# A hybrid decoder layer on one core: every fourth feed-forward weight tile gets its low part from an adding transfer

## The chip, the core and the metric

The kernel runs on one core of a Trainium2 chip. The metric is the device time of one execution in microseconds (us), lower being better. The engines are TensorE (PE; its weight loads are listed as PEld), VectorE (DVE), ScalarE (ACT), GpSimd (POOL) and SyncE (SP), which issues nearly all of the transfers. A transfer is carried out by 16 DMA engines that all queues share.

## The reference

One decoder layer over 256 tokens of width 2048, all in float32.

```
h = RMSNorm(x);  P = h @ W_in                  # pool channels (1024) | q | k | v (8 heads of 128 each)
A = pool_mixer(P_pool);  B = dilated_attention(q, k, v)
x = x + concat(RMSNorm(A), RMSNorm(B)) @ W_out
x = x + relu(RMSNorm(x) @ W_up)^2 @ W_down     # 8192 feed-forward columns
out = RMSNorm(x)
```

The feed-forward weights W_up and W_down are 64 MiB each, two thirds of what is read.

## The kernel before

**Products in three parts.** A float32 product a @ w runs as a_hi @ w_hi + a_lo @ w_hi + a_hi @ w_lo, where hi is the operand rounded to float32r and lo the exact rest. The activations' parts are made where the activations arise. The weights' parts are made tile by tile while the kernel runs.

**The weights' pipeline.** All weights are one list `order` of 176 tiles of 1 MiB (128 partitions x 2048 float32), in the order in which they are used: 32 for the input projection, 16 for the output projection, then four times 16 of W_up and 16 of W_down. A tile's index is t. Half a tile (128x1024) is one step s, with t = s // 2. In form B (used for W_up) a tile holds 8 row blocks of 256 columns and the weights are stationary; in form A (W_down) it holds 4 row blocks of 512 columns and the activations are stationary. Either way a step is 24 blocks of 512 columns' worth of products, or 8 pairs of a 512- and a 256-column product.

**The loop.** One Python loop goes over all the steps and writes the program of every engine. In iteration s it writes:

- `split(s + AHEAD)`, with `AHEAD` = 4: ScalarE rounds the half tile into `w_hi` (line 124), VectorE subtracts that from the raw half into `w_lo` (line 125). Both come from a pool with AHEAD + 1 = 5 buffers, so the high part of step s + 4 takes the buffer that the products of step s - 1 have just left.
- on even s, `load(s // 2 + RAW_AHEAD + 1)`, with `RAW_AHEAD` = 3: SyncE issues the transfer of a whole raw tile (line 108) into one of four buffers, once the tile that was in it has been split.
- `products(s)`: TensorE's products (lines 163 to 165 in form A, 169 and 171 in form B). In both forms the first product of a step reads `w_hi` and the second `w_lo`.
- the evacuation of an accumulator that is complete: for W_up `evac_up` by way of `joined` (lines 190, 192, 433, 435, 436, on ScalarE and VectorE in turn, every fourth step), for W_down `evac_down` (line 444, on VectorE, every eighth).

Each engine works through its program in the order written, and engines wait for each other by semaphores. Nothing is reordered.

**Buffers named `v0` and `v1`.** `v_parts`, the values of the attention, lie in the two buffers `v0` and `v1`. After the attention `v0` is used again for the gain of the last norm, `gfin` (lines 530 and 533), and `v1` for nothing more. GpSimd issues five small loads at the start (lines 68 to 500) and adds squares; it has nothing to do in the feed-forward part.

Of the kernel before, what the change touches and what calls it, by code (L numbers as in the profile page):

```python
# [8 lines left out]
F32R = mybir.dt.float32r  # L9
AF = mybir.ActivationFunctionType  # L10
OP = mybir.AluOpType
AX = mybir.AxisListType

P = 128
S = 256
# [17 lines left out]
@with_exitstack  # L33
def hybrid_block(ctx: ExitStack, tc: tile.TileContext, xT, x, w_v, w_qkp, w_out, w_up, w_down,
                 pool_w, pool_scale, g_mix, g_cat, g_mlp, g_final, ident_in, negdist_in, lncount_in, out):
    """Products of float32 operands a @ w run as a_hi @ w_hi + a_lo @ w_hi + a_hi @ w_lo, where hi is the
    operand rounded to float32r and lo the exact rest.  Form A keeps activations stationary and streams
    512 columns of weights (tokens on the output's partitions); form B keeps weights stationary and
    streams [a_hi | a_lo] (columns on the output's partitions)."""
    nc = tc.nc  # L40
    ctx.enter_context(tc.manual_schedule())

# [1 line left out]
    big = ctx.enter_context(tc.tile_pool(name="big", bufs=1))  # L44
    wraw = ctx.enter_context(tc.tile_pool(name="wraw", bufs=RAW_AHEAD + 1))
    wsplit = ctx.enter_context(tc.tile_pool(name="wsplit", bufs=AHEAD + 1))
    work = ctx.enter_context(tc.tile_pool(name="work", bufs=2))
# [4 lines left out]

    st = {}

    # ---- the scalar engine's square-root table, ahead of its first use
    warm = const.tile([P, 1], F32, name="warm")
    nc.vector.memset(warm, 1.0)
    nc.scalar.activation(warm, warm, AF.Sqrt)

    # ---- the tensor engine's clock comes up with work: products of zeros while the first loads are on their way  # L60
    zeros = const.tile([P, 256], mybir.dt.bfloat16, name="zeros")
    nc.vector.memset(zeros, 0.0)
    idle = ps_tp.tile([P, 256], F32, name="tp")
# [3 lines left out]
    gmix = const.tile([P, KT], F32, name="gmix")  # L67
    nc.gpsimd.dma_start(gmix, g_mix)

    # ---- operands in two parts: [row block, part, token]  # L70
    h_op = big.tile([P, KT, 2, S], F32R, name="h_op", tag="setA")
    xt = big.tile([P, KT, S], F32, name="xt", tag="setB")

# [3 lines left out]
                                       op0=OP.mult, op1=OP.subtract)  # L77

    def rsqrt_mean(ssq, n, name):
        """1 / sqrt(ssq / n + eps), with one Newton step behind the table's square root."""  # L80
        width = ssq.shape[-1]
        m = small.tile([P, width], F32, name=name + "_m", tag="rs_m%d" % width)
        nc.vector.tensor_scalar(m, ssq, 1.0 / n, EPS, op0=OP.mult, op1=OP.add)
        s = small.tile([P, width], F32, name=name + "_s", tag="rs_s%d" % width)
        nc.scalar.activation(s, m, AF.Sqrt)
        r0 = small.tile([P, width], F32, name=name + "_r0", tag="rs_r0%d" % width)
        nc.vector.reciprocal(r0, s)
        t = small.tile([P, width], F32, name=name + "_t", tag="rs_t%d" % width)
        nc.vector.tensor_tensor(t, r0, r0, op=OP.mult)
        nc.vector.tensor_tensor(t, t, m, op=OP.mult)  # L90
        nc.vector.tensor_scalar(t, t, -0.5, 1.5, op0=OP.mult, op1=OP.add)
        r = const.tile([P, width], F32, name=name)
        nc.vector.tensor_tensor(r, r0, t, op=OP.mult)
        return r

    # ---- the weights' pipeline: tiles of 1 MiB, split in halves
    order = []
    raws, splits, accs, tasks = {}, {}, {}, {}

    def load(t, pieces=1, of=None):  # L100
        if t >= len(order):
# [8 lines left out]
    def split(s, pieces=1, of=None, by_vector=False):  # L110
        t, half = divmod(s, 2)
        if t >= len(order):
            return
        src = raws[t][:, half * 1024:(half + 1) * 1024]
        if s not in splits:
            splits[s] = (wsplit.tile([P, 1024], F32R, name="w_hi"), wsplit.tile([P, 1024], F32R, name="w_lo"))
        hi, lo = splits[s]
        n = 1024 // pieces
        for i in of or range(pieces):
            c = slice(i * n, (i + 1) * n)  # L120
            if by_vector:
                nc.vector.tensor_copy(hi[:, c], src[:, c])
            else:
                nc.scalar.activation(hi[:, c], src[:, c], AF.Copy)  # L124
            nc.vector.tensor_tensor(lo[:, c], src[:, c], hi[:, c].bitcast(F32), op=OP.subtract)  # L125

    whole, halves = (slice(0, CA),), (slice(0, CA // 2), slice(CA // 2, CA))

    def cuts_of(key, tt):
        """The very last accumulator, of the second tile of tokens, comes in halves, each a tile by itself."""  # L130
        return halves if tt == 1 and key == order[-1]["key"] else whole

    def sums(key, tt, cut):
# [50 lines left out]
        tasks.setdefault(step, []).append((f, a))  # L184

    def joined(key):
        """Form B's sums: both halves of the accumulator together, [P, 2, S]."""
        acc = accs.pop(key)
        cross = work.tile([P, 2, S], F32, name="cross", tag="cross")
        nc.scalar.activation(cross, acc[:, :, S:], AF.Copy)  # L190
        z = work.tile([P, 2, S], F32, name="z", tag="z")
        nc.vector.tensor_tensor(z, acc[:, :, :S], cross, op=OP.add)  # L192
        return z

    # ---- input projection
    def square_x(n):
        """Squares of four row blocks, in the place of x, folded into one block and added to the others'."""
        t = xt[:, n * 4:n * 4 + 4]
        nc.scalar.activation(t, t, AF.Square)
        nc.gpsimd.tensor_tensor(t[:, :2], t[:, :2], t[:, 2:], op=OP.add)  # L200
        if n == 0:
            st["sq", "x"] = const.tile([P, S], F32, name="sq_x")
            nc.gpsimd.tensor_tensor(st["sq", "x"], t[:, 0], t[:, 1], op=OP.add)
        else:
            for i in range(2):
                nc.gpsimd.tensor_tensor(st["sq", "x"], st["sq", "x"], t[:, i], op=OP.add)  # L206
# [4 lines left out]
        nc.vector.tensor_scalar(st["rq"], st["r", "x"], SCALE, None, op0=OP.mult)  # L211

    def spread_rx():
        """The tokens' factors along the free dimension, on all partitions."""
        p = ps_tp.tile([P, S], F32, name="tp")
        for tt in range(TT):
            nc.tensor.transpose(p[:, tt * P:(tt + 1) * P], st["r", "x"][:, tt:tt + 1].to_broadcast([P, P]), ident)
        st["rrow"] = const.tile([P, S], F32, name="rrow")
        nc.vector.tensor_copy(st["rrow"], p)
# [83 lines left out]
        return st["y"]  # L303

    def squares(name, src, scale, first):
        """Sums of squares over row blocks, token by token, one sum to a partition."""
        if first:
            st["sq", name] = const.tile([P, S], F32, name="sq_" + name)
            nc.scalar.activation(st["sq", name], src, AF.Square, scale=scale)
        else:  # L310
            t = work.tile([P, S], F32, name="sqt", tag="sqt", bufs=1)
            nc.scalar.activation(t, src, AF.Square, scale=scale)
            nc.gpsimd.tensor_tensor(st["sq", name], st["sq", name], t, op=OP.add)
# [51 lines left out]
            base, f = {"p": (0, evac_pool), "q": (4, evac_qk), "k": (8, evac_qk)}[kind]  # L365
            add_b(lambda i, n=base + n: w_qkp[n, i], (kind, n), h_operand, f)

    # ---- output projection, of the two mixers by themselves, and the second norm's operand
    def load_rows():
        st["xr"] = [big.tile([P, D], F32, name="xr", tag="late%d" % tt) for tt in range(TT)]  # L370
        for tt in range(TT):
            nc.sync.dma_start(st["xr"][tt], x[tt * P:(tt + 1) * P, :])
# [50 lines left out]
        for c in range(4):  # L423
            add_a(lambda kq, c=c: w_out[c, kq], (name, c), kqs, y_op, evac_out)

    # ---- the feed-forward layer, 2048 of its columns at a time; the norm's factor, squared, comes last
    def evac_up(step, key):
        b, c = key[1:]
        if c == 0:
# [24 lines left out]
        for c in range(4):  # L454
            add_a(lambda kq, b=b, c=c: w_down[b, c, kq], ("d", b, c), range(4), lambda b=b: st["act", b], evac_down)

    # ---- start
    def load_xT(k0, n):
        nc.sync.dma_start(xt[:, k0:k0 + n], xT[:, k0:k0 + n, :])

# [15 lines left out]
    put_xT(0, 1)  # L476
    put_xT(1, 1)
    split(0, pieces=2, of=(1,))
    put_xT(2, 2)
    split(1, pieces=2)  # L480
# [60 lines left out]
    at(n_in + 68, halve_final)  # L541

    def finish(tt, cuts):
        """The last columns of a tile of tokens, and its final norm."""
        xr = st["xr"][tt]
        ss = st["ss2"][:, tt]
        base = D - CA
# [7 lines left out]
        last = ss[:, 2 + len(cuts):3 + len(cuts)]  # L555
        m = small.tile([P, 1], F32, name="m_end", tag="m_end")
        nc.vector.tensor_scalar(m, last, ss[:, 2:3], 1.0 / D, op0=OP.add, op1=OP.mult)
        s = small.tile([P, 1], F32, name="s_end", tag="s_end")
# [2 lines left out]
        nc.vector.reciprocal(r0, s)  # L561
        t = small.tile([P, 1], F32, name="t_end", tag="t_end")
        nc.vector.scalar_tensor_tensor(t, r0, r0, m, op0=OP.mult, op1=OP.mult)
        # -2 / sqrt(m): the gain carries -1/2
        r = small.tile([P, 1], F32, name="r_end", tag="r_end")
        nc.vector.scalar_tensor_tensor(r, t, -3.0, r0, op0=OP.add, op1=OP.mult)
        for n, (c0, c1) in enumerate(((0, 256), (256, 768), (768, 1280), (1280, 1536), (1536, 2048))):
# [8 lines left out]
            nc.sync.dma_start(out[tt * P:(tt + 1) * P, cols], xr[:, cols])  # L576

    def sum_early():
        """All of the final norm's sums but the last chunk's, with the epsilon."""
        ss = st["ss2"]  # L580
        nc.vector.tensor_tensor(ss[:, :, 2:3], ss[:, :, 2:3], ss[:, :, 1:2], op=OP.add)
        nc.vector.scalar_tensor_tensor(ss[:, :, 2:3], ss[:, :, 0:1], D * EPS, ss[:, :, 2:3], op0=OP.add, op1=OP.add)
# [4 lines left out]
    for s in range(n_steps - tail):  # L587
# [4 lines left out]
        t, half = divmod(s, 2)  # L592
# [6 lines left out]
            f(*a)  # L599
    assert not tasks  # L600

    # ---- the last products go by tiles of tokens, so that the first tile's norm and store run under the second's
    for s in range(n_steps - tail, n_steps):
        products(s, tts=(0,), drop=False)
    finish(0, whole)
# [57 lines left out]
```

## Time and profile before

| | |
|---|---|
| median of 2 runs | 1024.0 us (1022.86 and 1025.13) |
| span of the profiled execution | 1022.8 us; the page gives no other time of it |
| TensorE busy | 1007.7 us, 99% |
| VectorE busy | 626.1 us, 61% |
| ScalarE busy | 481.5 us, 47% |
| GpSimd busy | 30.9 us, 3% |
| moved by DMA | 194.26 MB, mean 190 GB/s |

The busy time of an engine says how much of the span it worked, with TensorE's ends modelled. Which engine sets the time is read from the chain that ended last and from the waits: the first follows the last instruction back through whatever released each step, the second adds up for each pair of instructions how long the one waited for the other.

### The profile page before, as it was taken

How to read it: one execution, taken by the hardware profiler on the slowest of the kernel's cores; microseconds unless marked ns; L12 is line 12 of the kernel's file. 1: busy time of each engine (PE TensorE's matmuls, PEld its weight loads, DVE VectorE, ACT ScalarE, POOL GpSimd, SP SyncE). 2: the span in 40 equal slices, each digit the busy share in tenths (PEclk: the TensorE clock that was granted, in tenths of full speed). 3: DMA queues.
4: the chain of work that ended last, by engine and by line, in shares of the span. 5: the costliest groups of instructions: out<-in, count | busy, mean ns of one | idle time of the engine just before them, and what ended most of it. 6: DMA issues, size and time to landing. Idle time of an engine off the chain costs nothing.

```text
span 1022.8 us, 12969 instructions
## 1 busy us (share of the span) xinstructions
PE 1007.7 (99%) x5208; PEld 858.8 (84%) x5208; DVE 626.1 (61%) x749; ACT 481.5 (47%) x612; POOL 30.9 (3%) x52
## 2 busy tenths in 40 slices
PE   9899999999999999999999999999999999999996
PEld 6788888888888888888888888888888888888886
DVE  7677866867676655555555545455655555565563
ACT  7456445464555445343444443444443434454442
POOL 2500010010000000000000000000000000000000
PEclk9899999999999999999999999999999999999999
DMA  9654454466455566555455555555555555555532
GB/s 333 243 207 174 138 201 170 160 234 219 165 183 188 177 221 220 189 186 202 170 201 186 186 206 186 187 188 184 202 173 197 206 185 186 186 186 198 178 118 83
DMA packets 30891, 194.26 MB, mean 190 GB/s; under 512 B 3504, under 2 KB 4576, under 8 KB 8304
## 3 DMA queue, kind: packets, MB, share of 16 engines
q1 hardware_dynamic: 30672, 193.34, 53.5%
q8 instruction: 41, 0.67, 0.3%
q0 software_dynamic: 160, 0.09, 0.1%
q14 instruction: 18, 0.15, 0.0%
HBM read 191.33 MB, written 2.10 MB: 189 GB/s over the span
## 4 chain that ended last, share of the span: by engine, by line
PE 95%; DMA 2%; POOL 2%; SPq 0%; ACT 0%; DVE 0%; issue 0%; DVEq 0%; POOLq 0%; ACTq 0%
PE acc L169 32%; PE acc L171 16%; PE acc L163 15%; PE acc L164 15%; PE acc L165 15%; DMA raw<-w_v_dram 1%; POOL sq_x L206 1%; POOL xt L200 1%; DMA xt<-xT_dram 1%; PE end L164 0%; PE end L165 0%; PE end L163 0%; PE tp L393 0%; PE tp L282 0%; PE sc L346 0%; PE sc L348 0%
## 5 line engine op out<-in xcount | busy, mean ns | idle before, releaser
L125 DVE TENSOR_TENSOR w_lo<-raw,w_hi 128x1024 fp32r<-128x1024 f32 (+1 forms) x360 | 431.6, 1215 | 258.6 <-ACT w_hi L124 258.6
L124 ACT ACTIVATE w_hi<-raw 128x1024 fp32r<-128x1024 f32 (+1 forms) x359 | 366.5, 1038 | 293.8 <-PE acc L165 184.1
L169 PE MATMUL acc<-x_op,w_hi 128*128 128x512 f32 x1024 | 360.4, 397 | 0.0
L171 PE MATMUL acc<-x_op,w_lo 128*128 128x256 f32 x1024 | 287.4, 281 | 0.0
L169 PEld LDWEIGHTS acc<-x_op,w_hi 128*128 128x128 f32 x1024 | 192.2, 188 | 46.5
L171 PEld LDWEIGHTS acc<-x_op,w_lo 128*128 128x128 f32 x1024 | 193.5, 189 | 0.2
L164 PE MATMUL acc<-w_lo,act 128*128 128x512 f32 x496 | 193.1, 389 | 0.0
L163 PE MATMUL acc<-w_hi,act 128*128 128x512 f32 x496 | 193.0, 389 | 0.0
L165 PE MATMUL acc<-w_hi,act 128*128 128x512 f32 x496 | 193.0, 389 | 0.0
L169 PE MATMUL acc<-h_op,w_hi 128*128 128x512 f32 x384 | 138.0, 402 | 0.0
L165 PEld LDWEIGHTS acc<-w_hi,act 128*128 128x128 f32 x496 | 93.1, 188 | 19.5
L163 PEld LDWEIGHTS acc<-w_hi,act 128*128 128x128 f32 x496 | 93.1, 188 | 19.1
L164 PEld LDWEIGHTS acc<-w_lo,act 128*128 128x128 f32 x496 | 93.1, 188 | 18.9
L171 PE MATMUL acc<-h_op,w_lo 128*128 128x256 f32 x384 | 108.3, 282 | 0.0
L169 PEld LDWEIGHTS acc<-h_op,w_hi 128*128 128x128 f32 x384 | 73.4, 191 | 16.7
L171 PEld LDWEIGHTS acc<-h_op,w_lo 128*128 128x128 f32 x384 | 73.7, 192 | 0.1
L190 ACT ACTIVATE cross<-acc 128x512 f32<-128x512 f32 x44 | 26.2, 596 | 67.0 <-PE acc L171 67.0
L192 DVE TENSOR_TENSOR z<-acc,cross 128x512 f32<-128x512 f32 x44 | 30.4, 691 | 42.6 <-ACT cross L190 42.6
L163 PE MATMUL acc<-w_hi,y_op 128*128 128x512 f32 x128 | 50.6, 396 | 0.0
L165 PE MATMUL acc<-w_hi,y_op 128*128 128x512 f32 x128 | 50.0, 390 | 0.0
L164 PE MATMUL acc<-w_lo,y_op 128*128 128x512 f32 x128 | 49.9, 390 | 0.0
L435 ACT ACTIVATE act<-z 128x512 fp32r<-128x512 f32 x32 | 20.3, 633 | 47.5 <-DVE z L433 47.5
(169 smaller groups left out, 613.6 us busy)
## 6 DMA issues: line engine op xcount, KB each, us to landing
raw<-w_up_dram SPq DMA_DIRECT2D x64, 1024.0 KB, 4.7
raw<-w_down_dram SPq DMA_DIRECT2D x64, 1024.0 KB, 4.8
raw<-w_qkp_dram SPq DMA_DIRECT2D x24, 1024.0 KB, 4.8
raw<-w_out_dram SPq DMA_DIRECT2D x16, 1024.0 KB, 4.8
raw<-w_v_dram SPq DMA_DIRECT2D x16, 256.0 KB, 5.4
raw<-w_v_dram SPq DMA_DIRECT2D x4, 1024.0 KB, 4.8
xr<-x_dram SPq DMA_DIRECT2D x2, 1024.0 KB, 9.1
xt<-xT_dram SPq DMA_DIRECT2D x7, 256.0 KB, 5.4
```

Source lines behind the costliest of these rows:

```text
L124: nc.scalar.activation(hi[:, c], src[:, c], AF.Copy)
L125: nc.vector.tensor_tensor(lo[:, c], src[:, c], hi[:, c].bitcast(F32), op=OP.subtract)
L163: nc.tensor.matmul(p, a_hi, hi[:, c], start=first, stop=False)
L164: nc.tensor.matmul(p, a_hi, lo[:, c], start=False, stop=False)
L165: nc.tensor.matmul(p, a_lo, hi[:, c], start=False, stop=last)
L169: nc.tensor.matmul(acc[:, b], hi[:, c], op[:, kt].rearrange("p a s -> p (a s)"), start=first, stop=False)
L171: nc.tensor.matmul(acc[:, b, S:], lo[:, c], op[:, kt, 0], start=False, stop=last)
L190: nc.scalar.activation(cross, acc[:, :, S:], AF.Copy)
L192: nc.vector.tensor_tensor(z, acc[:, :, :S], cross, op=OP.add)
L200: nc.gpsimd.tensor_tensor(t[:, :2], t[:, :2], t[:, 2:], op=OP.add)
L206: nc.gpsimd.tensor_tensor(st["sq", "x"], st["sq", "x"], t[:, i], op=OP.add)
L435: nc.scalar.activation(act[:, k, 0], z, AF.Copy)
```

## The change

For 32 tiles, those of the feed-forward layer with t % 4 == 1 (49, 53, ... 173), the low part is made in another way. When the first half is due to be split, ScalarE writes the negated rounding of the whole tile, 128x2048, into a buffer `w_rest` in the place `v1`. Then GpSimd issues a transfer from the weights in HBM that adds to what lies there: -hi + w = lo. It is one transfer of 1 MiB with rows of 2048 elements. The high part of each half is made by ScalarE as before, and the products read both halves of the low part from `w_rest`. VectorE does nothing for these tiles. There is one buffer `w_rest`. The raw tile is still loaded by SyncE, so these weights are read twice from HBM.

```diff
-    raws, splits, accs, tasks = {}, {}, {}, {}
+    raws, splits, accs, tasks, rest = {}, {}, {}, {}, {}
...
         src = raws[t][:, half * 1024:(half + 1) * 1024]
+        if order[t]["key"][0] in ("u", "d") and t % 4 == 1:
+
+            if half == 0:
+                rest[t] = big.tile([P, 2048], F32R, name="w_rest", tag="v1")
+                nc.scalar.activation(rest[t], raws[t], AF.Copy, scale=-1.0)
+                nc.gpsimd.dma_start(rest[t], order[t]["w"], accum_op=OP.add)
+            hi = wsplit.tile([P, 1024], F32R, name="w_hi")
+            nc.scalar.activation(hi, src, AF.Copy)
+            splits[s] = hi, rest[t][:, half * 1024:(half + 1) * 1024]
+            return
         if s not in splits:
```

The rest of the diff takes comments out and leaves empty lines in their place.

## Rows read from the trace of the kernel before

**Rows 1.** The page, busy us (share of the span) and instructions of each engine.
```profile
PE 1007.7 (99%) x5208; PEld 858.8 (84%) x5208; DVE 626.1 (61%) x749; ACT 481.5 (47%) x612; POOL 30.9 (3%) x52
```

**Rows 2.** The page, the chain that ended last, shares by engine.
```profile
PE 95%; DMA 2%; POOL 2%; SPq 0%; ACT 0%; DVE 0%; issue 0%; DVEq 0%; POOLq 0%; ACTq 0%
```

**Rows 3.** Waits of all engines: who waited for whom, us in total, times, longest.
```profile
PEld acc L164 <- DVE w_lo L125: 1.3, 3, 0.5
```

**Rows 4.** Groups by line: busy us, mean ns of one, idle before and its releaser.
```profile
L125 DVE TENSOR_TENSOR w_lo<-raw,w_hi 128x1024 fp32r<-128x1024 f32 (+1 forms) x360 | 431.6, 1215 | 258.6 <-ACT w_hi L124 258.6
L124 ACT ACTIVATE w_hi<-raw 128x1024 fp32r<-128x1024 f32 (+1 forms) x359 | 366.5, 1038 | 293.8 <-PE acc L165 184.1 <-PE acc L169 69.6 <-ACT w_hi L124 29.1
```

**Rows 5.** Timeline of ScalarE in an up-projection: start us, us, instruction, idle before.
```profile
506.27 2.00 ACT L124 ACTIVATE w_hi<-raw 128x1024 fp32r<-128x1024 f32 x2
509.23 1.06 ACT L124 ACTIVATE w_hi<-raw 128x1024 fp32r<-128x1024 f32 x1 [0.96 <-ACT w_hi L124]
512.07 1.06 ACT L124 ACTIVATE w_hi<-raw 128x1024 fp32r<-128x1024 f32 x1 [1.78 <-PE acc L169]
...
520.54 1.06 ACT L124 ACTIVATE w_hi<-raw 128x1024 fp32r<-128x1024 f32 x1 [0.97 <-ACT w_hi L124]
```

**Rows 6.** Timeline of ScalarE in a down-projection.
```profile
606.87 1.06 ACT L124 ACTIVATE w_hi<-raw 128x1024 fp32r<-128x1024 f32 x1 [1.66 <-PE acc L165]
609.59 1.06 ACT L124 ACTIVATE w_hi<-raw 128x1024 fp32r<-128x1024 f32 x1 [1.66 <-PE acc L165]
...
620.47 1.06 ACT L124 ACTIVATE w_hi<-raw 128x1024 fp32r<-128x1024 f32 x1 [1.66 <-PE acc L165]
```

**Rows 7.** Waits of SyncE's queue.
```profile
SPq L108 <- DVE w_lo L125: 871.3, 168, 10.9
```

**Rows 8.** Instructions of line 533: duration in ns (min, median, max), starts.
```profile
L533 ACT ACTIVATE gfin<-gfin x1: 1901/1901/1901, 406.2 to 406.2; 128x2048 f32<-128x2048 f32 x1
```

**Rows 9.** Timeline of GpSimd at the start of the run.
```profile
1.25 0.70 POOL L68 DMA_DIRECT2D gmix<-g_mix_dram  x1 [0.81 <-POOLq L655]
1.95 0.55 POOL L494 DMA_DIRECT2D ident<-ident_in_dram  x1
```

**Rows 10.** DMA issues: times, KB each, median us from issue to landing.
```profile
ident<-ident_in_dram POOLq DMA_DIRECT2D x1, 64.0 KB, 3.6
gmix<-g_mix_dram POOLq DMA_DIRECT2D x1, 8.0 KB, 3.4
```

**Rows 11.** Windows: busy us of each engine, granted clock, DMA share, GB/s.
```profile
509.00:515.00 6.00, 6.00 (x36) 5.19 (x35) 3.16 (x3) 2.17 (x3) 0.00 (x0) 1.00 0.52 175
515.00:521.00 6.00, 6.00 (x36) 5.20 (x35) 4.42 (x5) 3.55 (x5) 0.00 (x0) 1.00 0.48 175
```

**Rows 12.** Timeline of SyncE's queue in the same stretch.
```profile
509.74 0.33 SPq L108 DMA_DIRECT2D raw<-w_up_dram  x1
514.42 0.33 SPq L108 DMA_DIRECT2D raw<-w_up_dram  x1
521.05 0.33 SPq L108 DMA_DIRECT2D raw<-w_up_dram  x1
```

**Rows 13.** DMA queues: packets, MB, share of 16 engines' span.
```profile
q1 hardware_dynamic: 30672, 193.34, 53.5%
```

**Rows 14.** Timeline of TensorE around the one long wait near the start.
```profile
39.68 1.01 PE L318 MATMUL tp<-ones,sq_x 128*128 128x1 f32 x4 [4.25 <-POOL sq_x L206]
```

**Rows 15.** Windows near the start, columns as in rows 11.
```profile
40.00:41.00 1.00, 1.00 (x5) 1.00 (x5) 0.16 (x1) 0.07 (x1) 0.00 (x0) 0.50 1.04 442
...
45.00:46.00 1.00, 1.00 (x5) 0.90 (x4) 0.63 (x1) 0.09 (x1) 0.00 (x0) 0.50 0.00 0
46.00:47.00 1.00, 1.00 (x6) 0.83 (x5) 0.00 (x0) 0.97 (x1) 0.00 (x0) 0.82 0.00 0
...
5.00:10.00 5.00, 4.08 (x14) 2.19 (x13) 3.09 (x7) 2.96 (x7) 0.20 (x1) 1.00 0.96 304
```

## Prediction

> **What bounds the kernel now.** I read the page's busy table first: TensorE is busy 99% of the span, VectorE 61%, ScalarE 47%, GpSimd 3% [rows 1]. The chain that ended last is 95% TensorE [rows 2]. So an edit that takes work from VectorE can pay only where TensorE waits for VectorE, and the table of waits gives all of TensorE's waiting for a low part (w_lo) as 1.3 us, three times in the whole run [rows 3]. The groups by line show what the change takes hold of: a half tile costs ScalarE 1.04 us on average (1.06 in the feed-forward part) for the high part and VectorE 1.2 us for the low part [rows 4]; neither engine is late. What decides here is therefore not how much work an engine gets, but whether the new way of making w_lo is done when TensorE comes to it. I read that from a clock of the feed-forward stage.
>
> **The clock of the stage.** One step is half a tile. ScalarE's high part of a half is let go by the end of a step's products, so its starts mark the steps: 509.23 and 520.54 are four steps apart in an up-projection, 2.83 us each [rows 5]; in a down-projection 609.59 and 620.47, 2.72 us each [rows 6]. The split of a half is written four steps ahead of its products.
>
> **Removed.** In 32 tiles (numbers 49, 53, ... 173) both subtractions on VectorE: 64 x 1.2 = 77 us of an engine that is 61% busy. On the end of the kernel that is worth at most the 1.3 us of TensorE's waits [rows 3]. I count 0. The weight buffer of such a tile is free when ScalarE is done with it, not VectorE; SyncE waits for VectorE's subtraction before nearly each load, 871 us in all [rows 7], so the load behind it goes out some 1.2 us earlier. The loads have three tiles of lead, so this gains nothing.
>
> **Added on ScalarE.** One negated rounding of 128x2048 per tile. The one Copy of that size in the trace, on gfin, took 1.90 us [rows 8]. It stands ahead of the tile's own high part on ScalarE, and nothing that it must wait for is late: its buffer was last read by products six steps earlier, its raw tile landed long before. In the up-projection ScalarE has just finished two high parts at 506.27 + 2.00 = 508.27 and idles until 509.23 [rows 5], so the rounding runs from 508.27 to 510.17. What is queued behind it, the high part of the same half, then ends at 511.2 in place of 510.3, and is wanted at 520.4: free. The evacuation of an accumulator comes two steps later, so it isn't held up either. In the down-projection the rounding starts after the high part of 606.87, at 607.93, and ends at 609.83 [rows 6]. ScalarE gains 32 x 1.9 = 61 us, all under TensorE's work.
>
> **Added: the adding transfer, and when it must have landed.** GpSimd's queue is empty in this part of the run, so it issues some 0.1 us after the rounding: at 510.25, or at 609.95. TensorE's products of that tile begin four steps after 509.2, at about 520.45, and their second matmul reads w_lo. The transfer thus has 10.2 us from issue to landing (10.4 in the down-projection, and less ScalarE load). Both halves hang on one transfer, so the first half waits for all of it.
>
> How long it takes no row of this trace shows; I bound it. Fixed part: the GpSimd queue's first transfer of 8 KB took 3.4 us to land and the 64 KB one 3.6, of which GpSimd itself took 0.55 to 0.70 [rows 9, 10]; I take 3.4, some 2.6 ahead of the data and 0.8 behind (the split is my choice). Data part: an ordinary 1 MiB weight load occupies the 16 DMA engines for 0.52 x 6 = 3.1 us or 0.48 x 6 = 2.9, by the two stretches with one load each [rows 11]; I take 3.0. The adding transfer reads 1 MiB of weights and also the 1 MiB of rounded values that it adds to, and writes 1 MiB. Low end 3.0 (the second reading costs nothing), high end 9.0 (reading, reading and writing one after the other). I take 6.0, the time for the bytes read, since the loads show 3.0 for 1 MiB read and written at once, so writing runs beside reading.
>
> A sentence of the Trainium skill speaks against this change: Collectives: The Full Stack, section "The bandwidth ceiling: the fold count and why AG ≠ RS ≠ AR", says that a reducing transfer gets half the rate of a copy because it needs two source reads on the same ring, not because the adding takes cycles. By that rule the data part would be an estimated 6.0 us; no run here shows it yet, and without it the sum would stand on the middle of the two ends, the same 6.0.
>
> Contention: in those 10.2 us SyncE issues two weight loads, the ones of 509.74 and of 514.42, the second about 1.2 us earlier after the change [rows 12]. Data of the adding transfer starts at 510.25 + 2.6 = 512.85, when 1.05 us of the first load is left; the second brings 3.0 more.
> - Alone, as if loads gave way: 512.85 + 6.0 + 0.8 = 519.65, in time by 0.8 us.
> - Last of all: 512.85 + 1.05 + 3.0 + 6.0 + 0.8 = 523.7, late by 3.25 us.
> - Shared so that it moves two rows of reading for each row of a load: the first load ends 3.15 us later (adding: 2.1 done), the remaining 3.9 take 5.85: 521.85, and 0.8 behind, 522.65: late by 2.2 us.
>
> I take the last. TensorE has no work to put in between, as the program order is fixed, and nothing is won back later: **32 x 2.2 = 70 us**. The next tile of this kind comes 22 us later, so the stalls don't pile up. DMA engines are 53.5% busy with loads [rows 13]; 32 x 6 = 192 engine-us more is 19% of the span, so throughput isn't the limit; only the landing is.
>
> The profiled span of 1022.8 us has no other part outside it that I can see; the two timed runs are 1022.86 and 1025.13, median 1024.0. So 1024 + 70 = **1094 us**, 6.8% slower. Of the unknown terms alone the slower case runs from a stall of 0.65 (1045) to 3.25 and a little over (1128).
>
> **Rival 1: it lands in time, no change.** This is the one on the other side: the forecast falls with it. Its place is the landing against the 10.2 us, its price nothing. It decides at a data part of about 3.4 us if the loads go first (then the stall is under 0.65 us, and 32 of them are under 2%), and at 6.8 if they give way. For it: the engines are idle almost half the time, and the loads have slack. Against it: the two loads lie right on the window. Time 1022 to 1028.
>
> **Rival 2: the adding is far slower than its bytes.** With 9.0 of data a third load, that of 521.05, falls into it too: 512.85 + 1.05 + 3 + 3 + 9 + 0.8 = 529.7, late by 9.2 us if it comes last, 5.6 by the sharing above or less; 32 x 5.6 = 179. And a long wait takes TensorE's clock down: when it had stood still for 4.25 us ahead of its products at 39.68 [rows 14], the granted clock was 0.50 from 40 to 46 and 0.82 in the next microsecond [rows 15], which is a loss of about 6 x 0.5 = 3 us. With that, 32 x 8.6 = 275 us, 1300 us; if the clock holds, 1203. For it: nothing in the trace adds in a transfer, and the fixed part could also be longer for 1 MiB than for 8 KB. Against: rows of 8 KB are as long as those of the loads.
>
> **Rival 3: the clock falls already at 2 to 3 us of waiting.** Then the forecast's stall costs up to 3 us more each, at most 32 x 5.2 = 166 us, 1190. TensorE was idle for 0.92 us in all between 5 and 10, with the clock at 1.00 [rows 15]; of single gaps between that and 4.25 the rows show nothing.
>
> **Rival 4: faster.** VectorE's 77 us would have to be on the chain. By [rows 2, 3] they aren't; at most 1.3 us.
>
> **How the numbers follow.** Forecast (stall of 0.65 to 3.3 us, clock held) 0.46; in time 0.31; far slower adding 0.13; clock falling too 0.08; faster by something unseen 0.02. The two-in-ten that I leave out are most of rival 2 and the top of rival 3; the low end takes in rival 1. Range 1021 to 1180. About 2% is what a measurement can tell from no change, that is 1003.5 to 1044.5: faster 0.02, same 0.31, slower 0.67.
>
> **What would show it.** In the profile after: GpSimd with 32 DMA issues in the feed-forward part, HBM reading up by 32 MiB, VectorE down by about 77 us and ScalarE up by about 61. TensorE waiting in front of the first w_lo product of tiles 49, 53 and so on, with the transfer named as releaser, 2 us each; landing from issue of about 12 us. If the landing is under 10.2 us there is no wait, and I am wrong by the whole 70 us; if it is 15 us or more, rival 2 has it, and the granted clock in the stretch behind each wait tells rival 3. If the wait is on ScalarE's rounding and not on the transfer, my placing of the rounding in ScalarE's idle time is wrong.

## The result, and the profile after

The changed kernel takes 1100.47 us (median of 2 runs, 1095.92 to 1105.01) where the kernel before takes 1024.0: ratio 1.075, 95% interval 1.0722 to 1.0778. The profiled execution is the slower of the two; its span is 1103.2 us, 80.4 more than before.

The page's busy table and the first two lines of its chain, after, to be held against [rows 1, 2]:

```profile
PE 1032.8 (94%) x5208; PEld 871.9 (79%) x5208; DVE 547.9 (50%) x685; ACT 534.9 (48%) x644; POOL 58.5 (5%) x84
...
PE 47%; DMA 35%; ACT 8%; issue 5%; DVE 2%; POOL 1%; SPq 0%; ACTq 0%; DVEq 0%; POOLq 0%
DMA w_rest<-w_up_dram 18%; DMA w_rest<-w_down_dram 16%; PE acc L179 14%; PE acc L174 8%; PE acc L175 8%; PE acc L181 7%; PE acc L173 7%; ACT w_rest L119 5%; ACT w_hi L134 2%; DMA raw<-w_v_dram 1%; DVE z L202 1%; DVE z L443 1%; ACT cross L200 1%; POOL sq_x L216 1%; POOL xt L210 1%
```

VectorE gave up 78 us (77 worked out) and ScalarE took on 53 (61 worked out; its neighbouring instructions overlap by about 0.1 us in the trace, as the rows below show). What changed is the chain: the adding transfers hold a third of it, and ScalarE's rounding that each of them waits for another 5%. TensorE had 95% before.

The waits of TensorE, after, of its weight loads (PEld) and of its products (PE), in us in total, times, longest:

```profile
PEld acc L181 <- DMA w_rest<-w_up_dram: 39.3, 16, 3.5
PE acc L181 <- DMA w_rest<-w_up_dram: 34.3, 16, 3.2
PEld acc L174 <- DMA w_rest<-w_down_dram: 27.9, 15, 3.0
PE acc L174 <- DMA w_rest<-w_down_dram: 21.6, 15, 2.5
```

Of 32 transfers 31 were late. The weight loads waited for 67.2 us in all, 2.17 each. A weight load begins to wait while the product ahead of it still runs, so the time that TensorE really stood still is the products' wait: 55.9 us, 1.80 each. The 32nd transfer, at 1067.62, when no load was left beside it, landed in time. The issues by line (times, KB each, median us to landing) give the reason:

```profile
raw<-w_up_dram SPq DMA_DIRECT2D x64, 1024.0 KB, 5.7
raw<-w_down_dram SPq DMA_DIRECT2D x64, 1024.0 KB, 5.8
...
w_rest<-w_up_dram POOLq DMA_DIRECT2D x16, 1024.0 KB, 12.5
w_rest<-w_down_dram POOLq DMA_DIRECT2D x16, 1024.0 KB, 11.6
```

The adding transfer takes 12.5 or 11.6 us against a window of 10.0 to 10.8 (8.1 in the first two rounds), and the ordinary loads take 5.7 or 5.8 in place of 4.7 to 4.8, for which no engine waits in this part of the run. One round of it follows, in an up-projection. ScalarE's timeline, after (compare [rows 5]):

```profile
541.61 1.99 ACT L134 ACTIVATE w_hi<-raw 128x1024 fp32r<-128x1024 f32 x2
543.51 1.91 ACT L119 ACTIVATE w_rest<-raw 128x2048 fp32r<-128x2048 f32 x1
545.32 1.04 ACT L122 ACTIVATE w_hi<-raw 128x1024 fp32r<-128x1024 f32 x1
547.25 1.06 ACT L122 ACTIVATE w_hi<-raw 128x1024 fp32r<-128x1024 f32 x1 [0.90 <-PE acc L179]
```

The rounding takes the idle time between the high parts, as forecast, and takes 1.9 us. GpSimd's issue of the adding transfer in the same round:

```profile
545.71 0.86 POOL L120 DMA_DIRECT2D w_rest<-w_up_dram  x1 [24.42 <-ACT w_rest L119]
```

SyncE's weight loads around it:

```profile
545.08 0.33 SPq L108 DMA_DIRECT2D raw<-w_up_dram  x1
548.34 0.33 SPq L108 DMA_DIRECT2D raw<-w_up_dram  x1
556.17 0.33 SPq L108 DMA_DIRECT2D raw<-w_up_dram  x1
```

One load goes out 0.6 us ahead of the adding transfer, one 2.6 us behind it, and a third at 556.17, when TensorE already wants the low part. TensorE's timeline where it needs the low part:

```profile
555.43 0.39 PE L179 MATMUL acc<-x_op,w_hi 128*128 128x512 f32 x1
559.00 0.39 PE L181 MATMUL acc<-x_op,w_rest 128*128 128x256 f32 x1 [3.18 <-DMA w_rest<-w_up_dram]
...
560.11 0.63 PE L179 MATMUL acc<-x_op,w_hi 128*128 128x512 f32 x1
```

The step's first product, with the high part, runs; the second waits for 3.18 us. The 512-column product that took 0.39 takes 0.63 a microsecond later: the clock has come down. The windows of that round (columns as in rows 11):

```profile
556.00:559.00 3.00, 0.00 (x1) 0.01 (x1) 1.36 (x2) 0.62 (x1) 0.00 (x0) 1.00 0.91 339
559.00:563.00 4.00, 4.00 (x14) 3.46 (x15) 0.00 (x0) 0.00 (x0) 0.00 (x0) 0.58 0.45 166
563.00:567.00 4.00, 4.00 (x24) 3.40 (x23) 1.35 (x2) 1.66 (x2) 0.00 (x0) 0.99 0.13 23
```

The granted clock is 0.58 over four microseconds: most of them at 0.50, the lower of the two levels, 1.2 GHz. TensorE worked on 14 products in them and on 24 in the next four. I looked at the 6 us behind each of the 31 waits in the same way. Behind 12 of them the granted clock was 0.72, behind 19 it was 1.00; by the weight loads' waits, the shortest with a fall behind it was 2.13 us, the longest without one 2.83. Twelve times 6 us at 0.72 are 20 us lost. The busy table gives the same share of the 80.4 us from the other side: TensorE stood still for 55.9 us on these waits and was busy for 25.1 us longer than before (1032.8 against 1007.7), with as many products; the two make 81.0, and its other idle time fell by 0.6. So about 56 us are waits, and 20 to 25 are products that ran slowly after 12 of them, some 2 us for each fall.

### The profile page after: what moved, and what is told of

Read it like the earlier page. It is cut to its first block, busy times and chain, and to the rows that moved or that the text cites. A ratio compares the mean times of both kernels' runs of the same rounds, so it can differ in the third digit from the quotient of the medians.

```text
span 1103.2 us, 12967 instructions
## 1 busy us (share of the span) xinstructions
PE 1032.8 (94%) x5208; PEld 871.9 (79%) x5208; DVE 547.9 (50%) x685; ACT 534.9 (48%) x644; POOL 58.5 (5%) x84
## 4 chain that ended last, share of the span: by engine, by line
PE 47%; DMA 35%; ACT 8%; issue 5%; DVE 2%; POOL 1%; SPq 0%; ACTq 0%; DVEq 0%; POOLq 0%
DMA w_rest<-w_up_dram 18%; DMA w_rest<-w_down_dram 16%; PE acc L179 14%; PE acc L174 8%; PE acc L175 8%; PE acc L181 7%; PE acc L173 7%; ACT w_rest L119 5%; ACT w_hi L134 2%; DMA raw<-w_v_dram 1%; DVE z L202 1%; DVE z L443 1%; ACT cross L200 1%; POOL sq_x L216 1%; POOL xt L210 1%
## 5 line engine op out<-in xcount | busy, mean ns | idle before, releaser
L135 DVE TENSOR_TENSOR w_lo<-raw,w_hi 128x1024 fp32r<-128x1024 f32 (+1 forms) x296 | 353.3, 1213 | 258.7 <-ACT w_hi L134 258.6
L134 ACT ACTIVATE w_hi<-raw 128x1024 fp32r<-128x1024 f32 (+1 forms) x295 | 298.4, 1031 | 281.4 <-PE acc L175 167.2
L181 PE MATMUL acc<-x_op,w_lo 128*128 128x256 f32 x768 | 215.3, 280 | 0.0
L181 PEld LDWEIGHTS acc<-x_op,w_lo 128*128 128x128 f32 x768 | 145.1, 189 | 0.2
L174 PE MATMUL acc<-w_lo,act 128*128 128x512 f32 x372 | 144.8, 389 | 0.0
L181 PE MATMUL acc<-x_op,w_rest 128*128 128x256 f32 x256 | 78.4, 306 | 34.3 <-DMA w_rest<-w_up_dram 34.3
L122 ACT ACTIVATE w_hi<-raw 128x1024 fp32r<-128x1024 f32 x64 | 67.0, 1049 | 38.8 <-PE acc L175 24.4
L181 PEld LDWEIGHTS acc<-x_op,w_rest 128*128 128x128 f32 x256 | 53.5, 209 | 39.3 <-DMA w_rest<-w_up_dram 39.3
L174 PEld LDWEIGHTS acc<-w_lo,act 128*128 128x128 f32 x372 | 69.9, 188 | 14.3
L174 PE MATMUL acc<-w_rest,act 128*128 128x512 f32 x124 | 53.2, 429 | 21.6 <-DMA w_rest<-w_down_dram 21.6
## 6 DMA issues: line engine op xcount, KB each, us to landing
raw<-w_up_dram SPq DMA_DIRECT2D x64, 1024.0 KB, 5.7
raw<-w_down_dram SPq DMA_DIRECT2D x64, 1024.0 KB, 5.8
raw<-w_qkp_dram SPq DMA_DIRECT2D x24, 1024.0 KB, 4.8
raw<-w_out_dram SPq DMA_DIRECT2D x16, 1024.0 KB, 4.8
w_rest<-w_up_dram POOLq DMA_DIRECT2D x16, 1024.0 KB, 12.5
w_rest<-w_down_dram POOLq DMA_DIRECT2D x16, 1024.0 KB, 11.6
raw<-w_v_dram SPq DMA_DIRECT2D x4, 1024.0 KB, 4.8
```

The costliest lines, as they stand in the source:

```text
L122: nc.scalar.activation(hi, src, AF.Copy)
L174: nc.tensor.matmul(p, a_hi, lo[:, c], start=False, stop=False)
L181: nc.tensor.matmul(acc[:, b, S:], lo[:, c], op[:, kt, 0], start=False, stop=last)
```

## The experiments

Two theories: (A) all of the loss hangs on the landing of the adding transfer, which is late because it reads twice as much and shares the engines with loads; (B) something else that the change brings costs it: the rounding on ScalarE, GpSimd's queue, the traffic as such, or rows of 2048 elements. The edits are to the changed kernel.

**Without the transfer.**

```diff
                 nc.scalar.activation(rest[t], raws[t], AF.Copy, scale=-1.0)
-                nc.gpsimd.dma_start(rest[t], order[t]["w"], accum_op=OP.add)
```

> The adding transfers are left out: ScalarE still writes the negated rounding, VectorE still does nothing for these 32 tiles, and the products read the negated rounding as if it were the low part (so the output lacks the low parts of 32 weight tiles). Theory (all of the loss is the wait for the landing): the time of the kernel before, 1022 to 1027 us, no wait of TensorE on w_rest. Rival (the 1.9 us rounding on ScalarE, or its place ahead of the high part, costs some of it): 1035 us or more. Rival (VectorE's relief was worth something): under 1018 us.

Measured: 1024.08 us against 1023.25, ratio 1.0004 (0.9994 to 1.0014). ScalarE's extra rounding costs nothing, and VectorE's relief of 77 us is worth nothing. The whole loss is in the transfer.

**A copy in place of the adding.**

```diff
-                nc.gpsimd.dma_start(rest[t], order[t]["w"], accum_op=OP.add)
+                nc.gpsimd.dma_start(rest[t], order[t]["w"])
```

> The transfer of GpSimd's queue writes the weights over the rounding in place of adding them (the low part of 32 tiles is then the whole rounded weight, so the output is another one); same queue, bytes read from HBM, bytes written, start and waits. Theory (a second reading, 3.0 us of the engines, makes the adding transfer late): landing of 8.5 to 10 us instead of 12, TensorE's waits on w_rest under 5 us in all, 1022 to 1032 us. Rival (the queue of GpSimd, its 0.86 us issue and its fixed part are slow for 1 MiB, whatever is done with the data): landing still 11.5 to 12.5, 1085 to 1105 us.

Measured: ratio 0.9999 (0.999 to 1.0009), no wait on w_rest. Its issues, and the GpSimd queue's share of the engines:

```profile
q0 software_dynamic: 4768, 33.65, 8.6%
...
w_rest<-w_up_dram POOLq DMA_DIRECT2D x16, 1024.0 KB, 6.7
w_rest<-w_down_dram POOLq DMA_DIRECT2D x16, 1024.0 KB, 7.0
```

Beside the same loads a copy lands in 6.7 to 7.0 us, sooner even than I expected. The queue is not what is slow; the adding is. GpSimd also needs 0.53 us to issue the copy, not 0.86.

**Two steps earlier, and one.** The rounding and the adding transfer are taken out of `split` and written two steps ahead; for one step the call stands ahead of `split`, on odd s, with (s + 5) // 2.

```diff
+    def lower(t):
+        if t < len(order) and order[t]["key"][0] in ("u", "d") and t % 4 == 1:
+            rest[t] = big.tile([P, 2048], F32R, name="w_rest", tag="v1")
+            nc.scalar.activation(rest[t], raws[t], AF.Copy, scale=-1.0)
+            nc.gpsimd.dma_start(rest[t], order[t]["w"], accum_op=OP.add)
...
         if s % 2 == 0:
+            lower(s // 2 + 3)
             load(s // 2 + RAW_AHEAD + 1)
```

> The rounding and the adding transfer of a tile are written two steps (5.4 to 5.7 us) earlier; nothing else changes. Theory (the landing is late by 2 us against a window of 10.2 us): the window is then about 15.5 us against a landing of 12 to 13.5, no wait is left, 1022 to 1030 us. Rival (the adding transfers cost by the load that they put on the engines, or by delaying the weight loads): 1060 us or more, the waits moved to other instructions.

> The rounding and the adding transfer are written one step (2.7 to 2.8 us) earlier than in the changed kernel. Theory (the landing against the window, and a transfer that starts ahead of the loads lands sooner, as the one two steps earlier did with 9.2 us): the window grows to about 12 to 13 us and the landing is 9.5 to 11.5, so no wait or a few tenths, 1022 to 1035 us. Rival (the landing stays at 12.3, only the window moves): waits of up to 0.5 us, up to 1045 us.

Measured: two steps 1.0005 (0.9995 to 1.0014), one step 0.9994 (0.9984 to 1.0003), no wait in either. The traffic is all there and the loss is gone. The two runs are nearly one and the same, though. In iteration s the first writes the rounding behind `split(s + 4)`, and the second writes it in the next iteration ahead of `split(s + 5)`; for ScalarE that is one place, a single half tile ahead of the changed kernel's. GpSimd's timeline of the first, then of the second:

```profile
542.52 0.86 POOL L137 DMA_DIRECT2D w_rest<-w_up_dram  x1 [21.75 <-PE acc L181]
```

```profile
542.57 0.86 POOL L137 DMA_DIRECT2D w_rest<-w_up_dram  x1 [21.74 <-PE acc L181]
```

From issue to need it is 11.2 us in the up-projections and 13.1 in the down-projections (medians), in both, and not the 15.5 that I expected of two steps. So a step earlier was tried, and two were not. In the up-projections 11.2 us would still be too short for the changed kernel's 12.5: what saves them is that the landing itself got shorter, which I hadn't worked out ahead of the first of the two. The issues of the one called two steps earlier:

```profile
w_rest<-w_up_dram POOLq DMA_DIRECT2D x16, 1024.0 KB, 9.1
w_rest<-w_down_dram POOLq DMA_DIRECT2D x16, 1024.0 KB, 9.2
```

**One step later.** The rounding and the transfer go to the second half's split.

```diff
             if half == 0:
                 rest[t] = big.tile([P, 2048], F32R, name="w_rest", tag="v1")
+            else:
                 nc.scalar.activation(rest[t], raws[t], AF.Copy, scale=-1.0)
                 nc.gpsimd.dma_start(rest[t], order[t]["w"], accum_op=OP.add)
```

> The rounding and the adding transfer of a tile are written one step (2.7 to 2.8 us) later, so each wait is longer by about that. Theory (32 waits, the landing against the window, the clock held or lost for 3 us behind a wait): the wait goes from 2.1 to 4.5 or 5 us; with the clock held 32 x 2.7 = 86 us over the changed kernel, 1180 to 1190 us; with the clock at half behind every wait another 3 us each, 1260 to 1290 us. After waits of about 3 us some clocks fell in the changed kernel, so I expect the clock to fall behind most, 1230 to 1290 us. Rival (the loads are done meanwhile, so the landing gets shorter by what the start gets later): 1090 to 1120 us.

Measured: 1162.4 us, ratio 1.1359 (1.1336 to 1.1383), between the theory's numbers and the rival's. Its waits and its issues:

```profile
PEld acc L182 <- DMA w_rest<-w_up_dram: 55.1, 16, 4.6
PEld acc L175 <- DMA w_rest<-w_down_dram: 50.2, 16, 3.9
```

```profile
w_rest<-w_up_dram POOLq DMA_DIRECT2D x16, 1024.0 KB, 11.3
w_rest<-w_down_dram POOLq DMA_DIRECT2D x16, 1024.0 KB, 10.8
```

The weight loads' waits are 3.3 us, not 4.5 to 5: a good part of what the start got later came back by a landing that is about 1 us shorter, as the rival had it. The clock fell behind 24 of 32 waits, but a fall cost less than my 3 us: the span is 137.4 us over the one before, TensorE's products waited for 93.5 of them, and TensorE was busy for 1052.3 us, 44.6 more than before, 1.9 for each fall.

**The transfers alone.** The loads of the feed-forward tiles are left out.

```diff
+        if t >= 48:
+            raws[t] = raws[44 + t % 4]
+            return
         if t not in raws:
```

> SyncE's loads of the 128 feed-forward tiles are left out, the tiles' high parts are made from old raw tiles (so the output is another one); the adding transfers stay and have the DMA engines to themselves. Theory (6.0 us of data for 2 MiB read, made late by two loads): landing of 9.4 us (3.4 + 6.0), no wait on w_rest, 1020 to 1026 us. Rival (the adding itself is slow, the loads hardly matter): landing of 11 us or more, waits of 1 to 2 us, 1050 to 1090 us.

And the same with the copy in place of the adding:

> Both edits together: no feed-forward loads by SyncE (high parts from old raw tiles) and the transfer of GpSimd's queue overwrites in place of adding, so the output is another one. The adding transfer alone landed in 8.0 us with 5.9 us of the engines. Theory (the engines' time goes with the bytes read): a copy of the same 1 MiB alone takes 3.0 us of the engines and lands in 5 us. Rival (the converting path of this queue is slow by itself): 6.5 us or more. The time is 1020 to 1027 us by both.

Measured, one execution each: 1025.39 and 1025.05 us, with one wait of 0.5 us in the first and none in the second. The adding transfers alone (the queue's line, then the issues):

```profile
q0 software_dynamic: 4768, 33.65, 17.8%
...
w_rest<-w_up_dram POOLq DMA_DIRECT2D x16, 1024.0 KB, 8.0
w_rest<-w_down_dram POOLq DMA_DIRECT2D x16, 1024.0 KB, 8.0
```

The copies alone:

```profile
q0 software_dynamic: 4768, 33.65, 9.9%
...
w_rest<-w_up_dram POOLq DMA_DIRECT2D x16, 1024.0 KB, 5.0
w_rest<-w_down_dram POOLq DMA_DIRECT2D x16, 1024.0 KB, 5.0
```

One adding takes 17.8% of 1023.4 us by 32 = 5.7 us of the 16 engines (not the 5.9 of my expectation), one copy 9.9% of 1023.1 by 32 = 3.2. The adding costs 2.5 us of the engines, and the landing is longer by 3.0. That the 2.5 us are a second reading fits their size; the trace shows the time, not the reading. Alone the adding transfer would be in time by 2 us, and a copy is in time beside the loads: it takes both, the adding and the loads, to be late.

**Which load.** From tile 76 on one load of four is cut to 64 columns, and `gfin` serves as its tile: with 0 for r the load that goes out just ahead of the adding transfer in the changed kernel, with 1 the one behind it. A third run cuts the latter once more and keeps a reference to the raw tile until its split, which was to hold the buffer.

```diff
+        if t >= 76 and t % 4 == r:
+            nc.sync.dma_start(raws[t][:, :64], order[t]["w"][:, :64])
+            raws[t] = st["gfin"]
+            return
         n = 2048 // pieces
```

> From tile 76 on, the loads of the tiles with t % 4 == 0 are cut to 64 of 2048 columns (these tiles' weights are then another matrix, and so is the output). This is the load that goes out just ahead of the adding transfer. Theory (what is ahead in the engines' queues counts most): landing of 8.5 to 9.8 us for these, no wait behind, about 1040 us (the first seven adding transfers keep their waits). Rival (each of the two loads beside it costs the same 2 us): landing of about 10.3, still hardly a wait. The two are told apart by this landing against that of the run without the load behind.

> The same cut, on the loads of the tiles with t % 4 == 1, the ones that go out 2 to 3 us behind the start of the adding transfer (another output too). Theory (the load behind it costs less than the one ahead): landing of 10.5 to 11.5 us, waits of up to 1 us, 1040 to 1060 us. Rival (each costs the same): about 10.3. Opposite rival (the one behind costs more, because the queues share): 9.5 or less, no waits.

> The cut of the load behind once more (t % 4 == 1 from tile 76 on, 64 of 2048 columns, the tile's high part and rounding from the gain of the last norm), but with the raw buffer held until the tile is split. Without that hold the two runs before changed the order in which buffers come free, and their traces show no whole load ahead of the adding transfer in either: one load 2.8 us behind it (landing 8.5) and one 1.1 us behind it (9.4). Here one whole load goes out 0.6 to 0.8 us ahead of the adding transfer and none in the 9 us behind it. Theory (a load ahead puts the adding transfer back by more than one behind): landing of 10 to 11.5 us. Rival (one load costs 0.5 to 1.4 us wherever it is, only two together cost 4): 8.5 to 9.5 us.

Measured, one execution each: 1036.03, 1038.49 and 1037.92 us; most of the waits lie among the first six transfers, which keep both loads. The issues between 600 and 1030 us, in the first:

```profile
w_rest<-w_down_dram POOLq DMA_DIRECT2D x11, 1024.0 KB, 8.3
w_rest<-w_up_dram POOLq DMA_DIRECT2D x8, 1024.0 KB, 8.6
```

in the second:

```profile
w_rest<-w_down_dram POOLq DMA_DIRECT2D x11, 1024.0 KB, 9.6
w_rest<-w_up_dram POOLq DMA_DIRECT2D x8, 1024.0 KB, 9.2
```

and 9.6 and 9.3 in the third. But most of their rounds don't tell what I made them for. A tile that nobody reads gives its buffer to the next load at once, and so the loads around moved. SyncE's timeline in the second, where the adding transfer goes out at 713.40 (line 106 is the cut load, line 112 a whole one):

```profile
712.78 0.33 SPq L106 DMA_DIRECT2D raw<-w_up_dram  x1
714.50 0.33 SPq L112 DMA_DIRECT2D raw<-w_up_dram  x1
```

The whole load ahead of these, of 706.16, has landed by then, and another comes 1.1 us behind the adding transfer. In the first run one comes 2.8 us behind it, and the third repeats the second (1.1 us, after the cut load of 711.01), since the reference didn't hold the buffer. So from the second cut on all three have one whole load behind and none ahead: landing 8.3 to 8.6 us with the load 2.8 to 3.4 us behind, 9.2 to 9.6 with 0.8 to 1.1.

One round of the second run does show a load ahead alone, the first with a cut: there the buffers had not yet moved. Line 112 issued a whole load at 445.68, GpSimd the adding transfer at 446.49, 0.8 us behind it, and line 106 the cut load at 449.86; no other load follows before the landing. The issues of the whole load and of the adding transfer:

```profile
raw<-w_down_dram SPq DMA_DIRECT2D x1, 1024.0 KB, 5.7
w_rest<-w_down_dram POOLq DMA_DIRECT2D x1, 1024.0 KB, 10.6
```

The third run has the same round (443.14, 443.96, 447.32) with the same 10.6 us, and in the round before it, with all of the loads, both have 11.6.

What the runs show of contention: 8.0 us alone; 8.3 to 9.6 with one load behind; 9.1 with two behind, 1.9 and 3.7 us after it (two steps earlier, up-projection); 10.6 with one 0.8 us ahead; 12.5 with one 0.6 us ahead, one 2.6 behind and a third 10.5 behind (the changed kernel, up-projection; 11.6 in the down-projection). By these two rounds a load just ahead costs 2.6 us, more than two behind, which cost 1.1. What the second and the third load add is 1.0 us together in the down-projection; no run separates the third.

**Two halves.** One adding transfer for each half, rows of 1024.

```diff
-                nc.gpsimd.dma_start(rest[t], order[t]["w"], accum_op=OP.add)
+                for h in range(2):
+                    c = slice(h * 1024, (h + 1) * 1024)
+                    nc.gpsimd.dma_start(rest[t][:, c], order[t]["w"][:, c], accum_op=OP.add)
```

> The adding transfer is issued as two, one for each half tile, with rows of 1024 elements, first half first. Theory (the first half waits only because the transfer is one piece; the second half is wanted 2.8 us later): the first lands in 7 to 9 us against a window of 10.2, the second in 12.5 to 13.5 against 13, so waits of 0 to 0.5 us are left, 1022 to 1040 us. Rival (both pieces advance together on the engines, and the first lands hardly earlier than the whole): waits of 1 us or more, 1060 to 1100 us.

Measured: 1039.99 us, ratio 1.0159 (1.0143 to 1.0175), at the upper end. 22 waits of 19.9 us in all, none longer than 1.9, and the clock stayed at 1.00 behind each. In a round that I followed the halves landed in 8.3 and 13.7 us, each from its own issue (medians of all rounds 8.1 and 12.6): the first is now early, and all 22 waits are for the second.

**Rows of 512 elements.**

```diff
-                nc.gpsimd.dma_start(rest[t], order[t]["w"], accum_op=OP.add)
+                nc.gpsimd.dma_start(rest[t], order[t]["w"], accum_op=OP.add, max_dma_last_dim=2048)
```

> The adding transfer stays one piece, but its rows are cut to 512 elements (2 KB), four for each row of 2048. Theory (bytes read and the loads beside them set the landing): landing within 1 us of 12.3, 1085 to 1120 us, slightly later by a longer issue on GpSimd. Rival (the rows of 2048 elements are the slow thing, because a row must be read whole before it is added): landing 10.5 us or less, 1020 to 1060 us.

Measured: 1148.64 us, ratio 1.1228 (1.1196 to 1.126), over the upper end of what I expected; landing 13.0. The long rows aren't the cost; four times as many make it worse. GpSimd's issue of one of them:

```profile
558.51 1.28 POOL L120 DMA_DIRECT2D w_rest<-w_up_dram  x1 [26.13 <-ACT w_rest L119]
```

It is 0.42 us longer than the 0.86 above, of a landing longer by 0.7. The weight loads' waits are 93.9 us in place of 67.2, 0.9 more each, and the clock fell behind 17 of them.

No version beat the kernel before, and by the first experiment none can that only relieves VectorE of these 77 us: VectorE isn't on the path.

## Why the prediction was right

**VectorE's relief 0, ScalarE's rounding 0.** Right; the run without the transfer shows both together at 0.04%.

**The window.** Right: 10.2 us forecast, 10.0 to 10.8 measured but for two rounds. The rounding ended where forecast, and the wait was on the transfer. One reading was wrong without effect: the products that last read the buffer end 4.0 to 6.6 us ahead of the rounding, less than three steps and not six.

**The data part, 6.0 us of the engines.** 5.7 alone, right. The Trainium skill says in Collectives: The Full Stack, "The bandwidth ceiling: the fold count and why AG ≠ RS ≠ AR", that two source reads halve the rate. It says so of rings of several cores; the trace agrees in size, with 5.7 us against 3.2, a ratio of 1.8.

**The fixed part, 3.4 us.** Too long: 8.0 - 5.7 leaves 2.3. I took it from the queue's first transfers, at the start of the run. The packets in the trace of the transfers alone begin 1.6 us behind the issue, where I had 2.6, and end 0.3 ahead of the landing, where I had 0.8.

**Contention, 3.0 us (12.4 landing against 9.4 alone).** Too short: 12.5 - 8.0 = 4.5 in the up-projections, 11.6 - 8.0 = 3.6 in the down-projections. The two errors nearly cancel: 12.4 us forecast, 12.3 measured. That is luck: with the fixed part 1.1 us shorter and the rest as it was I would have forecast 1.1 us of stall and 1059. What I missed is that the data of the adding transfer starts only when the load that went out 0.6 to 0.8 us ahead of it is nearly done. DMA queues in the round shown, where q1 has SyncE's loads and q0 the adding transfer (packets, MB, share of the 16 engines), from 545 to 549.5 with no packet of q0, from 549.5 to 552, from 552 to 556 and from 556 to 559:

```profile
q1 hardware_dynamic: 123, 1.00, 75.5%
...
q0 software_dynamic: 53, 0.43, 92.4%
...
q0 software_dynamic: 67, 0.55, 65.8%
q1 hardware_dynamic: 61, 0.50, 30.9%
...
q1 hardware_dynamic: 129, 0.93, 78.4%
q0 software_dynamic: 24, 0.07, 11.1%
```

Issued at 545.71, it moves nothing until the load ahead is nearly done, then has the engines almost to itself, and then shares them two to one with the load behind, as the forecast had it. The median over all rounds is 3.7 us from issue to the first packet, against 1.6 alone, and 8.1 us from the first packet to the end of the last, against 6.1. So the place behind a load costs 2.1 us and the sharing 2.0. In the runs one step earlier, with both loads behind it in the up-projections, the first packet comes after 1.6 us. It doesn't end last of all, either: the load of 548.34 landed 0.9 us behind it.

```profile
raw<-w_up_dram SPq DMA_DIRECT2D x1, 1024.0 KB, 11.6
```

In all 31 late rounds that load landed 0.8 to 1.3 us behind the adding transfer, so the order of landing in the forecast was right.

**The stall, 32 x 2.2 = 70 us.** Too large: TensorE stood still for 55.9 us, 31 x 1.80. I counted from the start of the tile's products, but the first of them needs no low part and runs for 0.4 us; without it 2.2 is 1.8.

**Rival 3, the clock, chance 0.08.** I kept it apart from the forecast, which held the clock. It is part of the result, in 12 of 31 waits, at 20 to 25 us in all. Without it the profiled execution, 1105 us, would stand near 1080, with 56 us of waits in place of 70. That the forecast of 1094 lies so near to 1100 is therefore luck in part: a stall that was counted too long makes up for more than half of a clock that fell. The mechanism, a transfer that lands about 2 us late in 31 of 32 rounds, is what the runs show.

**Rivals 1 and 2.** In time: true of the copy, and of the adding one step earlier. Far slower: no; 5.7 us, not 9.0. The 5.6 us late of that rival is also a slip: by the sharing that it names, 9.0 of data take 13.5 us and are late by 6.7.

## What to carry to other kernels

Before moving a part of the work to a transfer, write down when it can start, when it is wanted, and which transfers lie beside it; an engine share of 54% says little about one landing. Where the landing just misses, look at the transfer that goes out just ahead: one step earlier the adding transfer went ahead of the loads, its landing fell by 2.4 to 3.4 us while its window grew by 0.9 to 2.5, and the 7.5% vanished; two halves left 1.6%. And ask first whether the engine that is relieved is on the path: here it wasn't, so the best outcome was no change.

## What the runs showed that I had not expected

- Where a transfer stands among others mattered more than how many there are: two loads behind it added 1.1 us to the landing, a single one 0.8 us ahead 2.6.
- TensorE's granted clock came down to 0.50 behind waits of a weight load as short as 2.13 us, though not behind every one: a wait of 2.83 us in the changed kernel, and one of 3.72 with rows of 512, left it at 1.00. The waits of two halves, up to 1.9 us, all left it at 1.00.
- GpSimd's issue depends on what the transfer does: 0.53 us for the copy, 0.86 for the adding, 1.28 for the adding with rows of 512.
